# A diffusion backbone layer on one core: the x tiles of the first head group turned to token-major by 32x32 blocks and transfers through DRAM, and its B tile projected last

## The chip, the cores and the metric

The kernel runs on one core of a Trainium2 chip. The core's engines work side by side, each through its own list of instructions: TensorE (matmuls), VectorE, ScalarE and GpSimd; SyncE's queue (SP) issues most transfers between DRAM and the on-chip memory SBUF. Matmuls write to PSUM, from which VectorE or ScalarE take the result. The metric is device microseconds per run; lower is better. An engine that waits for a semaphore holds back everything behind it in its list, and this is as true of the SP queue.

## The reference

One layer works on 512 latent tokens and 256 context tokens of width 1024. Both are normalized, modulated, and multiplied by one wide weight matrix; its columns feed a Mamba-2 mixer (SSD), a windowed attention, and gates. The two branches are merged, and a gated FFN with a convolution follows. What matters here is the SSD's input: columns x (2048, as 4 head groups of 512), B and C (4 groups of 128 states each) go through a convolution of width 3 along the tokens and SiLU.

```python
xbc = jax.nn.silu(dwconv_centred(xbc_raw, conv_w, conv_b))
xs = xbc[..., :D_SSD].reshape(Bsz, L, SSD_GROUPS, SSD_HPG, SSD_HEADDIM)
bm = xbc[..., D_SSD:D_SSD + D_BC].reshape(Bsz, L, SSD_GROUPS, SSD_STATE)
...
states = jnp.einsum('bcsgn,bgrcs,bcsgrp->bcgrpn', bc, decay_to_end, xc)
...
y_diag = jnp.einsum('bgrcls,bcsgrp->bclgrp', scores, xc)
y_off = jnp.einsum('bclgn,bcgrpn,bgrcl->bclgrp', cc, states[:, :-1], jnp.exp(cs))
```

The scan runs in both directions over 4 chunks of 128 latent tokens; it starts from the states that the context's 2 chunks leave. The sums over tokens (`s`) need x and B with tokens on the partitions.

## The kernel before, in words

Every projection is a float32 product made of three matmuls on rounded parts: a weight tile of 128 columns is loaded (`load_raw`, line 177, 512 KB, three buffers `wraw`), ScalarE casts it to the high part `whi` (line 183), VectorE subtracts to get the low part `wlo` (line 184; two buffers of each). `gemm` (lines 237, 238, 240) then multiplies high by high, high by low and low by high for each of 8 slices of the width. Its results have channels on the partitions and tokens along the row: `acc`, 128x512 for latent tokens and 128x256 for context.

For head group g, `proj_steps` makes one step each for B (`b_fn`), C (`c_fn`, latent tokens only) and four x tiles of 128 channels (`x_fn`, called x0 to x3 here). `conv_silu` does the convolution: ScalarE (line 1390), VectorE twice (1391, 1392), ScalarE's tanh (1398), VectorE (1399), all that in one pass for latent and one for context tokens. The result still has channels on the partitions. So each of its 128x128 blocks is turned by TensorE against the identity (`turn`, line 1418) into PSUM, and ScalarE copies the turned tile to `xs` or `xsc` (line 1462), or to `Bk` or `Bkc` for B (line 1439). The turns are not made at once: `TURN` is a list of tiles that wait for one, and `BETWEEN` a list of functions of which `gemm` calls one after every third slice, so that turns and the small matmuls of the scan fall in the middle of the next projection.

`ssd_steps` is the scan of a group. `states` first weighs the context tile `xsc` (line 1491, `xw`), multiplies it by `Bkc` (1520, the state matmuls), copies the state (1522), and then goes back through the latent chunks, where each `advance` (1503 on TensorE, 1505 on GpSimd, 1506 on VectorE) needs a weighed chunk of `xs`. `chunk_in` builds the decay tables E (1593 to 1602) from tables `fb` that are loaded from DRAM, `chunk_out` multiplies E by `xs` (1618). The program goes: projections of group 0; then, per group, its `states`, one gate projection (z15 here for group 0: matmuls, tanh at line 763, VectorE at 765, and a write to DRAM at 766), B of the next group (B1 here), four gate tiles loaded back (1553), a modulation tile m (loaded to `wraw`, used on VectorE at 793 and 795), C of the next group (C1), and the chunks with the x tiles of the next group between them.

In this part the order of the instructions on each engine is set by a scheduler when the program is built, not by the source alone. It is fixed after that. The SP queue's order is set in the same way. Farther on in the program a piece of code (line 1956) turns tiles by VectorE's block transpose and writes them to DRAM block by block (line 1959).

Of the kernel before, what the change touches and what calls it, by code (L numbers as in the profile page):

```python
# [9 lines left out]
F32 = mybir.dt.float32  # L10
# [8 lines left out]
P = 128  # L19
D = 1024  # L20
L = 512
LC = 256
# [22 lines left out]
def tile_hybrid_layer(  # L45
# [31 lines left out]
    nc = tc.nc  # L77
    V, S, G, T = nc.vector, nc.scalar, nc.gpsimd, nc.tensor
# [3 lines left out]
    hpool = ctx.enter_context(tc.tile_pool(name="hpool", bufs=1))  # L82
    tpool = ctx.enter_context(tc.tile_pool(name="tpool", bufs=2))
    dpool = ctx.enter_context(tc.tile_pool(name="dpool", bufs=1, space=DRAM))
# [11 lines left out]
    def bank(name):  # L96
        pool, w = banks_[name]
        return pool.tile([P, 512 * w], F32, tag=name, name=name)
# [8 lines left out]
    def accb():  # L107
        return bank("acc")

    def misb():  # L110
        return bank("mis")
# [3 lines left out]
    def tmp(tag):  # L115
        return tpool.tile([P, 512], F32, tag=tag, name=tag, bufs=TMP[tag])
# [27 lines left out]
    for j, t in enumerate((wdn[0], DSUMS[1], DSUMS[2], DSUMS[5], DSUMS[4], wdn[1], wdn[3])):  # L144
        for u in range(DU):
            n = min(2, DK - 2 * u) * HC
# [82 lines left out]
    BETWEEN = []  # L229

    def gemm(targets, w, nk=KT, m=P, k0=0, first=True, last=True, ks=None):
        hi, lo = w
        for k in range(nk) if ks is None else ks:
            wh, wl = hi[:, k * m : (k + 1) * m], lo[:, k * m : (k + 1) * m]
            a, b = first and k == 0, last and k == nk - 1
            for ps, xh, xl in targets:
                T.matmul(ps, wh, xh[:, k0 + k, :], start=a, stop=False)  # L237
                T.matmul(ps, wh, xl[:, k0 + k, :], start=False, stop=False)  # L238
            for ps, xh, xl in targets:
                T.matmul(ps, wl, xh[:, k0 + k, :], start=False, stop=b)  # L240
            if BETWEEN and k % 3 == 1:
                BETWEEN.pop(0)()
# [24 lines left out]
    dt_d = dpool.tile([64, L + LC], F32, name="dt_d")  # L267
    tt_d = dpool.tile([64, 4], F32, name="tt_d")
    x1_d = dpool.tile([L, D], F32, name="x1_d")
    g2_d = dpool.tile([D], F32, name="g2_d")  # L270

    def col(base, i):
# [152 lines left out]
    with tc.tile_pool(name="spool", bufs=1) as sp:  # L425
# [196 lines left out]
        def put(x, n):  # L622
            r[x] = in_sbuf(B_["s" + x], n, "r_" + x)
# [37 lines left out]
        r = {}  # L661
        cq = tmp("te")[:, :LC]
        for j in range(KT):
# [46 lines left out]
            x = ("hi", "lo") if j >= NU else ("hh", "hl")  # L710
# [31 lines left out]
        for n in range(2):  # L742
            for j in range(KT):
                x = ("hi", "lo") if j >= NU else ("hh", "hl")
# [642 lines left out]
    bp = bpool.enter_context(tc.tile_pool(name="bpool", bufs=1, reuse_waits="tile"))  # L1387

    def conv_half(ps, n, base_w, base_b, i, stride, o):
        S.activation(o[:, :n], ps[:, :n], AF.Identity, scale=hcol(base_w, stride + i), bias=hcol(base_b, i))  # L1390
        V.scalar_tensor_tensor(o[:, 1:n], ps[:, 0 : n - 1], hcol(base_w, i), o[:, 1:n], ALU.mult, ALU.add)  # L1391
        V.scalar_tensor_tensor(o[:, 0 : n - 1], ps[:, 1:n], hcol(base_w, 2 * stride + i), o[:, 0 : n - 1], ALU.mult, ALU.add)

    def conv_silu(ps, n, i, o):
        a = tmp("ta")
        conv_half(ps, n, V_CW, V_CB, i, 24, a)
        t = tmp("tb")
        S.activation(t[:, :n], a[:, :n], AF.Tanh)
        V.scalar_tensor_tensor(o[:, :n], t[:, :n], 1.0, a[:, :n], ALU.add, ALU.mult)

    def flat(a):
        return a.rearrange("p a b -> p (a b)")
# [7 lines left out]
    GR = [{} for _ in range(4)]  # L1410
    TURN = []

    def turn(n=None):

        for t, n_, put in TURN[:n]:
            ps = misb()
            for c in range(n_):
                T.transpose(ps[:, c * P : (c + 1) * P], t[:, c * P : (c + 1) * P], ident)
            put(ps)
        del TURN[:n]  # L1420

    def proj_steps(g):
        d = GR[g]

        def b_fn(w):
            d["xs"] = bp.tile([P, 4, 512], F32, tag="xs", name="xs", bufs=2)
            d["xsc"] = bp.tile([P, 2, 512], F32, tag="xsc", name="xsc", bufs=1)
            d["Bkc"] = bp.tile([P, 2, P], F32, tag="Bkc", name="Bkc", bufs=2)
            d["Bk"] = bp.tile([P, 4, P], F32, tag="Bk", name="Bk", bufs=2)
            d["BT"] = bp.tile([P, L], F32, tag="BT", name="BT", bufs=2)  # L1430
            pl, pc = accb(), accb()
            gemm([LAT(pl)], w)
            turn()
            gemm([CTX(pc)], w)
            conv_silu(pl, L, 16 + g, d["BT"])
            BTc = tmp("tc")
            conv_silu(pc, LC, 16 + g, BTc)
            for t, n, k in ((d["BT"], 4, d["Bk"]), (BTc, 2, d["Bkc"])):
                TURN.append((t, n, lambda ps, n=n, k=k: S.copy(flat(k), ps[:, : n * P])))

        def c_fn(w):
            d["CT"] = bp.tile([P, L], F32, tag="CT", name="CT", bufs=2)
            pl = accb()
            gemm([LAT(pl)], w)
            turn(1)
            conv_silu(pl, L, 20 + g, d["CT"])

        def x_fn(ct, w):
            i = 4 * g + ct
            pl, pc = accb(), accb()  # L1450
            gemm([LAT(pl)], w)
            if not BETWEEN:
                BETWEEN.extend([lambda: None, lambda: turn(1), turn])
            gemm([CTX(pc)], w)
            for pp, n, dst in ((pl, L, d["xs"]), (pc, LC, d["xsc"])):
                xl = tmp("tc")
                conv_silu(pp, n, i, xl)
                TURN.append(
                    (
                        xl,  # L1460
                        n // P,
                        lambda ps, n=n, dst=dst: S.copy(
                            dst[:, :, ct * P : (ct + 1) * P], ps[:, :n].rearrange("p (a b) -> p a b", b=P)
                        ),
                    )
                )

        r = [([("x", 16 + g)], b_fn), ([("x", 20 + g)], c_fn)]
        for ct in range(4):
            r.append(([("x", 4 * g + ct)], lambda w, ct=ct: x_fn(ct, w)))  # L1470
        return r

    SQUARES = []

# [176 lines left out]

    msteps = [m_step(i) for i in range(32)]
    prog = proj_steps(0)
    for g in range(4):
        s = ssd_steps(g)
        f = fill[n2 + g : n2 + 1 + g]
        b = proj_steps(g + 1) if g < 3 else fill[n2 + 4 : n3]
        m = msteps[2 * g : 2 * g + (4 if g == 3 else 2)]

        prog += s[0:1] + f + b[0:1] + s[1:2] + s[10:11] + m[0:1] + b[1:2]  # L1660
        for c in range(4):
            prog += s[2 + 2 * c : 4 + 2 * c] if c < 3 else s[8:9]
            prog += b[2 + c : 3 + c]
            if c == 1:
                prog += b[6:]
            if c == 1 or g == 3:
                prog += m[1 + c : 2 + c] if g == 3 else m[1:2]
        prog += s[9:10]
# [86 lines left out]
    q2 = hpool.tile([P, L], F32, name="q2")  # L1755
# [522 lines left out]
```

## Time and profile before

| | us |
|---|---|
| median of 3 runs (range) | 1220.63 (1220.55 to 1221.63) |
| profiled execution, time | 1221.22 |
| profiled execution, span | 1219.4 |
| TensorE busy | 1211.3 |
| VectorE busy | 924.5 |
| ScalarE busy | 684.4 |
| GpSimd busy | 182.3 |

The sum of busy times is far above the span, since the engines work side by side. A row of the time order has the start, the length, the engine, the source line, the operation and its operands with output first. A row of the groups ends with the total and the mean (in ns), then the idle time before these instructions and what ended it. Lines are those of the kernel before; in the changed kernel the same lines stand one lower from line 270 on, and 28 to 37 lower in and behind the changed functions.

### The profile page before, as it was taken

What the parts mean: (1) busy time and instruction counts of PE and PEld (TensorE: products, weight loads), DVE (VectorE), ACT (ScalarE), POOL (GpSimd) and SP (SyncE); (2) the same over time, 40 slices, a digit from 0 to 9 for tenths busy, and PEclk for the clock granted to TensorE, in tenths of its full rate; (3) what the DMA queues carried; (4) which work ended last, traced back from release to release, by engine and by line L of the source; (5) the groups of instructions that cost most, each with busy time, mean ns of one, the idle gap of its engine ahead of it and who ended that gap; (6) DMA issues with size and microseconds to landing.
All of it is one profiled execution on the core that took longest, in us unless ns stands there. A gap on an engine that the chain in (4) does not pass through costs nothing.

```text
span 1219.4 us, 17443 instructions
## 1 busy us (share of the span) xinstructions
PE 1211.3 (99%) x6320; PEld 995.9 (82%) x6320; DVE 924.5 (76%) x1491; ACT 684.4 (56%) x1271; POOL 182.3 (15%) x183
## 2 busy tenths in 40 slices
PE   9999999999999999999999999999999999999997
PEld 6798888888878877778787778888988888888886
DVE  5857888888564698697896867677687877778778
ACT  5657787788544457476575664223544343436653
POOL 0000121100000043262451632000200000000021
PEclk9999999999999999999999999999999999999999
DMA  9645889844756335357366568777265534336662
GB/s 368 260 138 184 160 242 260 171 149 126 176 160 162 111 117 164 128 125 203 97 159 204 155 209 281 217 248 240 51 162 147 179 115 139 112 122 228 194 182 96
DMA packets 121383, 211.55 MB, mean 173 GB/s; under 512 B 25672, under 2 KB 67728, under 8 KB 121296
## 3 DMA queue, kind: packets, MB, share of 16 engines
q1 hardware_dynamic: 110256, 187.09, 49.4%
q0 software_dynamic: 10752, 23.07, 8.5%
q8 instruction: 50, 0.82, 0.3%
q14 instruction: 37, 0.30, 0.1%
q10 hardware_dynamic: 288, 0.27, 0.1%
HBM read 185.68 MB, written 42.28 MB: 187 GB/s over the span
## 4 chain that ended last, share of the span: by engine, by line
PE 96%; DVE 1%; issue 1%; ACT 1%; DMA 1%; POOL 0%; SPq 0%; POOLq 0%; DVEq 0%; ACTq 0%
PE acc L237 20%; PE acc L240 20%; PE acc L238 20%; PE score L957 3%; PE po L1006 3%; PE pt L993 2%; PE mis L579 2%; PE mis L1610 2%; PE mis L1503 2%; PE mis L1618 1%; PE mis L2137 1%; PE mis L2138 1%; PE mis L2139 1%; PE acc L2137 1%; PE acc L2139 1%; PE acc L2138 1%
## 5 line engine op out<-in xcount | busy, mean ns | idle before, releaser
L183 ACT CAST whi<-wraw 128x1024 fp32r<-128x1024 f32 (+1 forms) x115 | 120.6, 1049 | 158.0 <-PE acc L238 109.5
L184 DVE TENSOR_TENSOR wlo<-wraw,whi 128x1024 fp32r<-128x1024 f32 (+1 forms) x115 | 144.6, 1258 | 68.7 <-ACT whi L183 65.0
L237 PE MATMUL acc<-hlh,whi 128*128 128x512 f32 x472 | 194.2, 411 | 0.0
L238 PE MATMUL acc<-hll,whi 128*128 128x512 f32 x472 | 185.0, 392 | 0.0
L240 PE MATMUL acc<-hlh,wlo 128*128 128x512 f32 x472 | 184.9, 392 | 0.0
L237 PE MATMUL acc<-mh,whi 128*128 128x512 f32 x368 | 143.6, 390 | 0.0
L238 PE MATMUL acc<-ml,whi 128*128 128x512 f32 x368 | 143.2, 389 | 0.0
L240 PE MATMUL acc<-mh,wlo 128*128 128x512 f32 x368 | 143.2, 389 | 0.0
L240 PEld LDWEIGHTS acc<-hlh,wlo 128*128 128x128 f32 x472 | 88.6, 188 | 19.5
L237 PEld LDWEIGHTS acc<-hlh,whi 128*128 128x128 f32 x472 | 88.8, 188 | 17.9 <-issue 3.1
L238 PEld LDWEIGHTS acc<-hll,whi 128*128 128x128 f32 x472 | 88.9, 188 | 17.4 <-issue 2.4
L237 PEld LDWEIGHTS acc<-mh,whi 128*128 128x128 f32 x368 | 69.1, 188 | 14.5
L238 PEld LDWEIGHTS acc<-ml,whi 128*128 128x128 f32 x368 | 69.1, 188 | 14.3
L240 PEld LDWEIGHTS acc<-mh,wlo 128*128 128x128 f32 x368 | 69.1, 188 | 14.2
L1391 DVE SCALAR_TENSOR_TENSOR ta<-acc,half,ta 128x511 f32<-128x511 f32 (+1 forms) x66 | 43.9, 666 | 26.3 <-ACT ta L1390 26.0
L966 DVE CUSTOM_DVE_ANT_0 p<-score,winm,nsink 128x512 f32<-128x512 f32 (+1 forms) x64 | 51.9, 811 | 15.3 <-PE score L957 13.8
L1390 ACT ACTIVATE ta<-acc,half 128x512 f32<-128x512 f32 (+1 forms) x66 | 46.9, 710 | 22.1 <-PE acc L240 20.8
L973 ACT ACTIVATE p<-p,mneg 128x512 f32<-128x512 f32 (+1 forms) x64 | 49.8, 778 | 15.4 <-DVE mneg L966 14.8
L237 PE MATMUL acc<-hch,whi 128*128 128x256 f32 x176 | 54.7, 311 | 0.0
L1505 POOL TENSOR_TENSOR st<-st,eT 128x512 f32<-128x512 f32 x24 | 29.8, 1243 | 165.3 <-ACT st L1522 151.9
L164 POOL DMA_DIRECT2D dsum<-wdn x24 | 25.4, 1144 | 193.0 <-DVE wlo L1090 171.7
L795 DVE SCALAR_TENSOR_TENSOR tm<-wraw,csil,tm 128x512 f32<-128x512 f32 x56 | 44.1, 787 | 13.1 <-DMA wraw<-wm 12.5
(440 smaller groups left out, 2998.2 us busy)
## 6 DMA issues: line engine op xcount, KB each, us to landing
wraw<-wup SPq DMA_DIRECT2D x44, 512.0 KB, 3.7
dsum<-wdn POOLq DMA_DIRECT2D x24, 704.0 KB, 8.5
fb<-cs_d SPq DMA_DIRECT2D x32, 512.0 KB, 6.5
wraw<-wm SPq DMA_DIRECT2D x32, 512.0 KB, 3.9
wraw<-wx SPq DMA_DIRECT2D x24, 512.0 KB, 3.5
wm<-wm SPq DMA_DIRECT2D x16, 512.0 KB, 8.1
wraw<-wz SPq DMA_DIRECT2D x16, 512.0 KB, 3.9
wraw<-wos SPq DMA_DIRECT2D x16, 512.0 KB, 4.8
```

The costliest lines, as they stand in the source:

```text
L183: F["cast"] = S.copy(hi[:, :n], r[:, :n])
L184: return V.tensor_tensor(lo[:, :n], r[:, :n], raw(hi[:, :n]), ALU.subtract)
L237: T.matmul(ps, wh, xh[:, k0 + k, :], start=a, stop=False)
L238: T.matmul(ps, wh, xl[:, k0 + k, :], start=False, stop=False)
L240: T.matmul(ps, wl, xh[:, k0 + k, :], start=False, stop=b)
L795: V.scalar_tensor_tensor(acc, r[:, u * 512 : u * 512 + 512], sc, acc, ALU.mult, ALU.add)
L957: T.matmul(ps[:, o : o + len(z) * P], Q[h][:, b * P : (b + 1) * P], k[:, j, z[0] * P : (z[-1] + 1) * P], start=v == 0 and o % 512 in (0, P ...
L966: V.tensor_tensor_reduce(p[:, :w], d["ps"][i][:, o0 : o0 + w], m, op0=ALU.add, op1=ALU.min, scale=1.0, scalar=nsink[:, h : h + 1], accum_o ...
L973: S.activation(p, p, AF.Exp, bias=d["mneg"][:, i : i + 1], scale=-1.0, accum_out=d["den"][:, i : i + 1])
L1006: T.matmul(d["po"], vst[:, cols[x], j, :], d[y][x], start=x == 0 and y == "pth", stop=x == c - 1 and y == "ptl")
L1390: S.activation(o[:, :n], ps[:, :n], AF.Identity, scale=hcol(base_w, stride + i), bias=hcol(base_b, i))
L1391: V.scalar_tensor_tensor(o[:, 1:n], ps[:, 0 : n - 1], hcol(base_w, i), o[:, 1:n], ALU.mult, ALU.add)
```

## The change

Group 0's x tiles are no longer turned by TensorE. VectorE transposes each convolved tile within blocks of 32x32 (`blocks_out`). Four transfers per tile, one for each 32 channels, write the blocks to a DRAM tensor `xs_d` of tokens by channels. Two loads per tile bring it back as `xs` and `xsc` (`blocks_in`, called in the middle of the next steps for the tiles that are ready). The transfers go out on the SP queue. The steps of group 0 get another order, so that x3 isn't last: x0, C, x1, x2, x3, B in place of B, C, x0 to x3. Groups 1 to 3 stay as they are.

```diff
+    xs_d = [dpool.tile([L + LC, 512], F32, name="xs_d%d" % g) for g in range(4)]
...
+    BY_BLOCKS = (0,)
+
+    def blocks_out(g, ct, n0, n, x):
+
+        t = hpool.tile([P, L], F32, tag="q2" if n == L else "rbc4", name="xb")[:, :n]
+        V.transpose(t, x[:, :n])
+        for a in range(4):
+            c = ct * P + 32 * a
+            o = xs_d[g][n0 : n0 + n, c : c + 32].rearrange("(f i) j -> i f j", i=32)
+            nc.sync.dma_start(o, t[32 * a : 32 * a + 32, :].rearrange("i (f j) -> i f j", j=32))
+
+    def blocks_in(g):
+
+        for ct in READY:
+            c = slice(ct * P, (ct + 1) * P)
+            for x, n0, n in ((GR[g]["xsc"], L, LC), (GR[g]["xs"], 0, L)):
+                nc.sync.dma_start(x[:, :, c], xs_d[g][n0 : n0 + n, c].rearrange("(a p) c -> p a c", p=P))
+        del READY[:]
...
         def b_fn(w):
-            d["xs"] = bp.tile([P, 4, 512], F32, tag="xs", name="xs", bufs=2)
-            d["xsc"] = bp.tile([P, 2, 512], F32, tag="xsc", name="xsc", bufs=1)
+            if not blocks:
+                x_tiles()
...
             gemm([LAT(pl)], w)
             turn()
+            blocks_in(g)
             gemm([CTX(pc)], w)
...
             pl = accb()
+            blocks_in(g)
             gemm([LAT(pl)], w)
             turn(1)
...
         def x_fn(ct, w):
             i = 4 * g + ct
             pl, pc = accb(), accb()
+            if blocks and not ct:
+                x_tiles()
+            blocks_in(g)
             gemm([LAT(pl)], w)
-            if not BETWEEN:
+            if not BETWEEN and not blocks:
                 BETWEEN.extend([lambda: None, lambda: turn(1), turn])
             gemm([CTX(pc)], w)
             for pp, n, dst in ((pl, L, d["xs"]), (pc, LC, d["xsc"])):
                 xl = tmp("tc")
                 conv_silu(pp, n, i, xl)
+                if blocks:
+                    blocks_out(g, ct, 0 if n == L else L, n, xl)
+                    continue
...
+            if blocks:
+                READY.append(ct)
...
-        return r
+        return [r[2], r[1], *r[3:], r[0]] if blocks else r
```

The scheduler's order shifts with it at three places. On the SP queue, this is where the weights of z15 (`wz`) and of B1 (the next `wx`) are asked for before:

```order
L1574 DMA fb_4886<-cs_d_100 128x8x128
L177 DMA wraw_4295<-wx 128x1024
L177 DMA wraw_4377<-wz 128x1024
L177 DMA wraw_4459<-wx 128x1024
L177 DMA wraw_4509<-wm2 128x1024
L1553 DMA zs_4653<-zs_d_97 128x512 x4
L177 DMA wraw_4658<-wx 128x1024
```

And in the changed kernel from x3's last writes on, where `xb_4383` is x3's latent tile and `xb_4397` its context tile, `wraw_4479` holds B1's weights and `wraw_4678` C1's:

```order
L1432 DMA xs_d0_104<-xb_4397 32x8x32 x4
L1439 DMA xs_4028<-xs_d0_104 128x4x128
L177 DMA wraw_4479<-wx 128x1024
L1439 DMA xsc_4029<-xs_d0_104 128x2x128
L767 DMA zs_d_97<-te_4526 128x512
L177 DMA wraw_4529<-wm2 128x1024
L1590 DMA zs_4673<-zs_d_97 128x512 x4
L177 DMA wraw_4678<-wx 128x1024
```

B1's weights now stand behind the block writes of x3 and a load back, and C1's behind z15's gate write, the modulation tile and the gate tiles.

On ScalarE, before, `whi_4461` is B1's high part and `tb_4504` z15's tanh:

```order
L183 CAST whi_4461<-wraw_4459 128x1024
L1462 COPY xsc_4023<-mis_4439 128x2x128
L1390 ACTIVATE ta_4452<-acc_4384,half_90 128x256
L1462 COPY xs_4022<-mis_4472 128x4x128
L1398 ACTIVATE tb_4456<-ta_4452 128x256
L1462 COPY xsc_4023<-mis_4487 128x2x128
L183 CAST whi_4660<-wraw_4658 128x1024
L763 ACTIVATE tb_4504<-acc_4465 128x512
```

In the changed kernel, with `whi_4481` for B1 and `tb_4524` for z15:

```order
L1399 ACTIVATE tb_4476<-ta_4472 128x256
L1467 COPY Bkc_4409<-mis_4507 128x256
L764 ACTIVATE tb_4524<-acc_4485 128x512
L183 CAST whi_4481<-wraw_4479 128x1024
L1559 COPY st_4547<-mis_4544 128x512
```

The cast of B1's weights has moved from well ahead of z15's tanh to right behind it.

On VectorE, the changed kernel between x3 and B1, where `ta_4464` is the convolution of B's latent part, `xb_4397` x3's context tile, `wlo_4482` B1's low part and `tm_4684` the modulation sum:

```order
L1428 STREAM_TRANSPOSE xb_4383<-tc_4375 128x512
L1392 SCALAR_TENSOR_TENSOR ta_4464<-acc_4412,half_90,ta_4464 128x511
L1393 SCALAR_TENSOR_TENSOR ta_4464<-acc_4412,half_90,ta_4464 128x511
L1428 STREAM_TRANSPOSE xb_4397<-tc_4389 128x256
L1400 SCALAR_TENSOR_TENSOR BT_4411<-tb_4468,ta_4464 128x512
...
L766 SCALAR_TENSOR_TENSOR te_4526<-tb_4524,acc_4485 128x512
L1528 TENSOR_TENSOR xw_4520<-xsc_4029,TD_3666 128x512
L184 TENSOR_TENSOR wlo_4482<-wraw_4479,whi_4481 128x1024
L1528 TENSOR_TENSOR xw_4522<-xsc_4029,TD_3666 128x512
L794 TENSOR_SCALAR tm_4684<-wraw_4529,csil_89 128x512
```

Before, the same engine had this there (`wlo_4462` is B1's low part, `wlo_4661` C1's):

```order
L184 TENSOR_TENSOR wlo_4462<-wraw_4459,whi_4461 128x1024
L1391 SCALAR_TENSOR_TENSOR ta_4452<-acc_4384,half_90,ta_4452 128x255
L1392 SCALAR_TENSOR_TENSOR ta_4452<-acc_4384,half_90,ta_4452 128x255
L1399 SCALAR_TENSOR_TENSOR tc_4451<-tb_4456,ta_4452 128x256
L1491 TENSOR_TENSOR xw_4500<-xsc_4023,TD_3662 128x512
L1491 TENSOR_TENSOR xw_4502<-xsc_4023,TD_3662 128x512
L184 TENSOR_TENSOR wlo_4661<-wraw_4658,whi_4660 128x1024
L765 SCALAR_TENSOR_TENSOR te_4506<-tb_4504,acc_4465 128x512
```

x3's context tile is turned behind B's latent convolution, and B1's low part, formerly made ahead of all products on `xsc`, now stands behind the first of them. Beside these places, TensorE's first state matmul for group 0 stands after B1's second matmul and the other one after its fifth (both were after the sixth), C1's low part stands ahead of the first product on `xs`, and two VectorE steps on a later modulation tile, formerly among the first products on `xs`, stand in the first chunk: one ahead of the E products and one between the two.

More of the change, by code (lines that the diff above doesn't have):

```diff
@@ L1420, in turn, with x_tiles, b_fn @@
         del TURN[:n]
+    BY_BLOCKS = (0,)
[12 more added lines that the diff above has]
+        del READY[:]
+    READY = []
     def proj_steps(g):
         d = GR[g]
-        def b_fn(w):
+        blocks = g in BY_BLOCKS
+        def x_tiles():
             d["xs"] = bp.tile([P, 4, 512], F32, tag="xs", name="xs", bufs=2)
             d["xsc"] = bp.tile([P, 2, 512], F32, tag="xsc", name="xsc", bufs=1)
+        def b_fn(w):
+            if not blocks:
+                x_tiles()
             d["Bkc"] = bp.tile([P, 2, P], F32, tag="Bkc", name="Bkc", bufs=2)
```

## The prediction

> **What bounds the kernel now.** I read the page's busy times first, then the chain that ended last, then the stretch that the change touches, engine by engine.
>
> ```profile
> PE 1211.3 (99%) x6320; PEld 995.9 (82%) x6320; DVE 924.5 (76%) x1491; ACT 684.4 (56%) x1271; POOL 182.3 (15%) x183
> PE 96%; DVE 1%; issue 1%; ACT 1%; DMA 1%; POOL 0%; SPq 0%; POOLq 0%; DVEq 0%; ACTq 0%
> 365.85:421.92 56.07, 56.07 (x320) 48.97 (x318) 30.49 (x44) 27.53 (x52) 0.00 (x0) 1.00 0.50 144
> ```
>
> The first two lines are the busy times and the shares of the chain. TensorE is the bound, and the chain runs through it for 96% of the span. The third is the busy time of each engine in one stretch: its length, then PE, PEld, DVE, ACT and POOL, the granted clock, the DMA share and GB/s. The stretch reaches from the first matmul of the B tile of group 0 to the first of the B tile of group 1 (B1 below). TensorE is busy through all of it at full clock. So a TensorE instruction removed there saves its time, and a TensorE wait added there costs its time; work on VectorE (30.49 of 56.07 us) or ScalarE costs only what it makes TensorE wait.
>
> **What TensorE loses.** The change takes 24 of the 30 turns of 128x128 in this stretch (four channel tiles, four latent and two context blocks each); B's own six stay. Their price comes from the lengths of tiles without turns in the order of time on TensorE:
>
> ```profile
> 365.85 0.39 PE L237 MATMUL acc<-hlh,whi 128*128 128x512 f32 x1
> 371.32 0.28 PE L237 MATMUL acc<-hch,whi 128*128 128x256 f32 x1
> 374.19 0.40 PE L237 MATMUL acc<-hlh,whi 128*128 128x512 f32 x1
> 379.66 0.60 PE L1418 MATMUL mis<-ident,BT 128*128 128x128 f32 x4
> 421.92 0.39 PE L237 MATMUL acc<-hlh,whi 128*128 128x512 f32 x1
> ```
>
> B or x (latent and context part) takes 374.19 - 365.85 = 8.34 us, a latent part alone 379.66 - 374.19 = 5.47 us. The stretch holds five of the first (B, x0 to x3) and two of the second (C and z15): 41.70 + 10.94 = 52.64 us. The remaining 56.07 - 52.64 = 3.43 us are the 30 turns, 0.114 us each, so 24 are 2.74 us. That is the most that can be gained, 0.22%. Without any wait B1 would start at 421.92 - 2.74 = 419.18; call this moment T. The four and four copies out of PSUM (L1462) leave ScalarE, which has 28 us of slack there: nothing.
>
> **What the new road costs.** The kernel has the same road elsewhere already: line 1956 turns a tile in 32x32 blocks on VectorE and line 1959 writes it in four transfers of 64 KB. Its rows are the turn, the issue on the SP queue (min/median/max ns), the time from issue to landing, and the landing of other transfers:
>
> ```profile
> L1956 DVE STREAM_TRANSPOSE te<-x 128x512 f32<-128x512 f32 x8 | 5.6, 704 | 0.0
> L1959 SPq DMA_DIRECT2D x_d<-te x32: 303/480/1637, 865.9 to 940.9; - x32
> DMA to landing us min/median/max: 1.7/3.7/4.8
> wraw<-wx SPq DMA_DIRECT2D x24, 512.0 KB, 3.5
> wraw<-wm SPq DMA_DIRECT2D x32, 512.0 KB, 3.9
> zs<-zs_d SPq DMA_DIRECT2D x16, 256.0 KB, 4.5
> zs_d<-te SPq DMA_DIRECT2D x16, 256.0 KB, 2.6
> khi<-khi SPq DMA_DIRECT2D x6, 192.0 KB, 3.0
> ```
>
> VectorE gains four turns of 0.70 us and four of half the width (0.35 to 0.45, an estimate from the same row), 4.4 us in a stretch where it idles 25 us: hidden by that idle time. The SP queue gains 32 writes and 8 loads back, 40 x 0.48 = 19 us of issue, and each load back stops the queue until its block writes have landed. What is queued behind them are weight loads. Those for B and z15 are issued late but find room: before, the queue asked for B1's weights 24 us ahead of their cast, as the next rows show. The end of x3 has no such room.
>
> ```profile
> 391.10 0.33 SPq L177 DMA_DIRECT2D wraw<-wx  x1
> 415.55 1.04 ACT L183 CAST whi<-wraw 128x1024 fp32r<-128x1024 f32 x1
> 422.85 0.59 ACT L763 ACTIVATE tb<-acc 128x512 f32<-128x512 f32 x1
> 371.52 0.78 ACT L1390 ACTIVATE ta<-acc,half 128x512 f32<-128x512 f32 x1
> 373.12 0.75 DVE L1392 SCALAR_TENSOR_TENSOR ta<-acc,half,ta 128x511 f32<-128x511 f32 x1
> ```
>
> *B1's weights.* Before, they were cast (L183) 6 us before use. Now the cast stands behind z15's gate activation (L763) on ScalarE, and that waits for z15's last matmul. ScalarE starts 0.20 us after TensorE's last matmul of a tile (371.32 to 371.52), so B1's first matmul cannot start before T + 0.20 + 0.59 + 1.04 = T + 1.83 us. The order of the instructions forces this wait; it takes two thirds of the gain.
>
> *The context tile xsc.* Now VectorE's split of B1's weights (wlo) stands behind the first product on xsc (L1491). So follow xsc. The context block turn of x3 stands behind both convolution steps of B's latent part. That part ends a context part (374.19 - 371.32 = 2.87), z15 (5.47) and six turns (0.69) before T: T - 9.03. Convolution ends 373.12 + 0.75 - 371.32 = 2.55 later, the turn 0.4 after it: T - 6.1. The fourth write is issued three times 0.48 and 0.1 later, T - 4.5. It lands by the rows of x_d 1.7, 3.7 or 4.8 us later. Then the load back is issued, 128 KB, by the nearest rows 3.0 (khi) to 4.5 us (zs), 3.5 in the middle. So xsc is there at T + 0.2, T + 2.7 or T + 4.8.
>
> ```profile
> L1491 DVE TENSOR_TENSOR xw<-xsc,TD 128x512 f32<-128x512 f32 x16 | 10.6, 690 | 4.4 <-ACT xsc L1462 3.8 <-PE mis L1520 0.3
> L184 DVE TENSOR_TENSOR wlo<-wraw,whi 128x1024 fp32r<-128x1024 f32 x112 | 141.5, 1263 | 65.8 <-ACT whi L183 62.2 <-PE mis L1503 2.2 <-PE mis L1618 0.7
> 422.14 0.39 PE L238 MATMUL acc<-hll,whi 128*128 128x512 f32 x1
> 423.28 1.88 PE L1520 MATMUL mis<-xw,Bkc 128*128 128x512 f32 x4
> 424.59 0.79 PE L237 MATMUL acc<-hlh,whi 128*128 128x512 f32 x1
> 425.23 0.40 PE L238 MATMUL acc<-hll,whi 128*128 128x512 f32 x1
> 430.87 1.02 PE L1503 MATMUL mis<-xw,Bk 128*128 128x512 f32 x2
> ```
>
> Middle: 2.7 + 0.69 (product) + 1.23 (the split here; its mean is 1.26) = T + 4.6. The first matmul that needs wlo is B1's third, now with one state matmul ahead of it: 0.46 for two matmuls, (424.59 - 423.28) / 2 = 0.65 for the state, 0.41 for the matmul after an f32 one (425.23 - 424.59 = 0.64 in place of 422.14 - 421.92 = 0.22): T + 1.5 if nothing waited. Wait 3.1 us, which takes in the 1.83 above. The ends: T + 0.2 leaves the 1.83 alone; T + 4.8 makes it 5.2. I take the middle, since 3.7 is the median over 32 writes of the same form. The two state matmuls are now apart, so that one more matmul pays the step after f32: +0.41.
>
> *C1's weights* come next on the SP queue, behind z15's gate write, a modulation tile (m) and four gate tiles:
>
> ```profile
> 399.92 0.33 SPq L177 DMA_DIRECT2D wraw<-wm  x1
> 400.30 1.84 SPq L1553 DMA_DIRECT2D zs<-zs_d  x4
> 404.76 13.45 SPq L177 DMA_DIRECT2D wraw<-wx  x3
> 403.46 0.49 DVE L793 TENSOR_SCALAR tm<-wraw,csil 128x512 f32<-128x512 f32 x1 [1.69 <-DMA wraw<-wm]
> ```
>
> The gate's VectorE step ends at about T + 1.6; then 0.4 for each issue, and C1's load is issued at T + 4.3 (m and zs took 400.30 + 1.84 - 399.92 = 2.2 us). It comes after 1.5 MB and lands 3.5 us later by its own row, or up to 5.5 (an estimate: the 4.5 of zs, behind which it is queued, and 1 us more), T + 7.8 to T + 9.8. Cast, split and the product of the third chunk follow on ScalarE and VectorE: + 1.05 + 1.26 + 0.69 = T + 10.8 to T + 12.8. That product feeds the first advance of the state (L1503), due without waits at T + 430.87 - 421.92 + 0.41 = T + 9.36. Wait 1.4 to 3.4 us; it doesn't add to the 3.1, since it is counted from T too: the later of the two decides. The m tile lands about T + 6, and its two VectorE steps (0.49 and 0.75) end before the third state matmul is due with the wait of 3.1: nothing.
>
> *VectorE in the first chunk.* Two steps on the next m tile (L795) fell before into a wait of VectorE for data (second row). Now they stand ahead of and between the products on E (L1602), with no idle time to take them:
>
> ```profile
> 436.44:446.38 9.94, 9.94 (x55) 7.03 (x54) 9.77 (x17) 7.85 (x17) 3.49 (x4) 1.00 0.36 107
> 428.35 0.75 DVE L795 SCALAR_TENSOR_TENSOR tm<-wraw,csil,tm 128x512 f32<-128x512 f32 x1 [2.35 <-DMA wraw<-wm]
> 442.49 1.50 DVE L1602 TENSOR_TENSOR E<-E,mis 128x512 f32<-128x512 f32 x2
> 444.25 1.09 PE L1618 MATMUL mis<-E,xs 128*64 128x128 f32 x16
> ```
>
> VectorE is busy 9.77 of 9.94 us there (first row). They push the second E by 2 x 0.75 = 1.5 us. Before, it was ready at 443.99 and first used half way through the 16 matmuls, at 444.8: 0.8 us of room. TensorE itself is later by the sum so far and VectorE by a little less, so 0 to 0.9 us are lost; I take 0.5.
>
> **The sum**, against the profiled execution (span 1219.4, time 1221.22, 0.6 above the median 1220.63 of the runs): -2.74 + 3.1 + 0.41 + 0.5 = +1.3 us. On the median that is 1221.9 us. From the ends: -2.74 + 1.83 + 0.41 = -0.5, or 1220.1; -2.74 + 5.2 + 0.41 + 0.9 = +3.8, or 1224.4. A measurement of this kernel can tell about 0.2%, 2.4 us, from no change.
>
> **Rivals.** *All hidden:* weights and xsc are in time, the 2.74 us stay, 1217.9. For it speaks that the DMA engines have room; against it the cast behind the gate, which costs 1.83 whatever lands when. Chance 4%.
>
> *Slower, by landing times:* the place is the last block write of x3 and the load back. If together they take over 8.4 us (7.2 in the forecast), xsc comes after T + 3.9, and the wait exceeds 4.3, which is what turns the sum above +2.4. At the rows' maximum it gives 1224.4. For it: 4.8 was reached in x_d, and the load back is queued right behind B1's 512 KB. Against it: the engines are otherwise little used there.
>
> ```profile
> 407.00:415.00 8.00, 8.00 (x49) 7.09 (x48) 4.66 (x7) 3.25 (x6) 0.00 (x0) 1.00 0.31 102
> ```
>
> The DMA share before is 0.31 in this stretch. Chance 36%.
>
> *Strided writes one after another:* if the four writes of a tile do not overlap, the last lands 3 x 4.8 = 14 us later and the sum is 14 us worse than its middle, 1236. Against it, writes of x_d were issued 0.48 apart and none took over 4.8. Chance 2%. [...]
>
> **How the numbers follow.** The forecast, with xsc between T and T + 3.9 and so a change of -0.5 to +2.4 us, has the remaining 58%; its time is 1221.9. Faster by over 0.2% is the first rival alone, 0.04. Slower by over 0.2% is the second and third, 0.38. The rest, 0.58, lies within. The range goes from 1219.9, just below the forecast's lower end, to 1224.9, above the second rival's end; outside lie the first and third rival and a tail of the second.
>
> **What would show it.** In the changed profile: L1418's successor with 24 fewer turns by B1's start; ScalarE's gate and then the cast right before B1; TensorE idle 2 to 4 us at B1's first three matmuls, with VectorE's wlo or xw named; xw waiting for the DMA into xsc; a second wait, if any, at the first advance, put down to C1's wraw; block writes landing in 2 to 5 us. It is wrong if B1 waits under 1.8 us, if xsc lands after T + 5, if weights of B or z15 come late too, or if the time is lost or gained outside 365 to 450 us.

## The result, and the profile after

The changed kernel takes 1226.05 us (median of 6 runs, 1224.3 to 1227.1), the kernel before beside it 1220.68 us. The ratio is 1.0041, with a 95% interval of 1.0028 to 1.0054: slower by 0.41%, 1.15 us above the upper end of my range. The profiled execution took 1225.21 us (span 1223.4), 3.99 us more than the profiled one of before.

The first two lines are the busy times and the shares of the chain, from the page of the changed kernel. The third is the same stretch as in the prediction: from the first matmul of group 0's first projection (B before, x0 now) to the first of B1.

```profile
PE 1210.0 (99%) x6296; PEld 993.3 (81%) x6296; DVE 925.4 (76%) x1499; ACT 679.5 (56%) x1263; POOL 183.7 (15%) x183
PE 93%; ACT 2%; DVE 2%; DMA 1%; issue 1%; POOL 0%; SPq 0%; POOLq 0%; DVEq 0%; ACTq 0%
366.12:421.26 55.14, 53.52 (x295) 46.30 (x293) 31.13 (x49) 24.75 (x44) 0.00 (x0) 1.00 0.59 146
```

TensorE has 24 instructions less and 1.3 us less to do, yet its share of the chain fell from 96 to 93%, and VectorE's and ScalarE's rose from 1 to 2% each. The stretch is only 0.93 us shorter than before (55.14 for 56.07) though 2.74 us of turns are gone: it now ends with a wait of 1.62 us, 1.78 when counted from T (below). The waits of TensorE from 360 to 480 us (engine and line that waits, what for, total, times, longest); before, there was none in these 120 us:

```profile
PE mis L1540 <- DVE xw L1528: 2.1, 1, 2.1
PE acc L237 <- ACT whi L183: 1.6, 1, 1.6
PE mis L1557 <- DVE xw L1528: 1.4, 1, 1.4
```

Line 1540 is the advance of the state, 1557 the state matmuls, 1528 the products on xsc and xs. How they come about is read from four engines, in the order of time. First the SP queue, where 1432 is a block write, 1439 a load back, 767 z15's gate write and 1590 the gate tiles:

```profile
409.95 5.14 SPq L1432 DMA_DIRECT2D xs_d<-xb  x7
415.26 0.38 SPq L1439 DMA_DIRECT2D xs<-xs_d  x1
415.68 0.50 SPq L177 DMA_DIRECT2D wraw<-wx  x1
416.34 0.36 SPq L1439 DMA_DIRECT2D xsc<-xs_d  x1
421.02 0.33 SPq L767 DMA_DIRECT2D zs_d<-te  x1
421.40 0.43 SPq L177 DMA_DIRECT2D wraw<-wm  x1
421.87 2.07 SPq L1590 DMA_DIRECT2D zs<-zs_d  x4
424.05 3.98 SPq L177 DMA_DIRECT2D wraw<-wx  x3
```

B1's weights are asked for at 415.68, 24.6 us later than before (391.10); C1's are the first of the three at 424.05, 19.3 us later than before (404.76). Then ScalarE and VectorE:

```profile
419.68 0.60 ACT L764 ACTIVATE tb<-acc 128x512 f32<-128x512 f32 x1 [1.72 <-PE acc L240]
420.17 1.04 ACT L183 CAST whi<-wraw 128x1024 fp32r<-128x1024 f32 x1
430.63 1.05 ACT L183 CAST whi<-wraw 128x1024 fp32r<-128x1024 f32 x1 [5.16 <-DMA wraw<-wx]
420.31 0.69 DVE L766 SCALAR_TENSOR_TENSOR te<-tb,acc 128x512 f32<-128x512 f32 x1 [3.66 <-ACT tb L764]
420.92 0.68 DVE L1528 TENSOR_TENSOR xw<-xsc,TD 128x512 f32<-128x512 f32 x1
425.95 0.94 DVE L794 TENSOR_SCALAR tm<-wraw,csil 128x512 f32<-128x512 f32 x1 [2.61 <-DMA wraw<-wm]
427.59 1.29 DVE L1528 TENSOR_TENSOR xw<-xsc,TD 128x512 f32<-128x512 f32 x2
431.71 1.22 DVE L184 TENSOR_TENSOR wlo<-wraw,whi 128x1024 fp32r<-128x1024 f32 x1 [2.83 <-ACT whi L183]
432.85 2.15 DVE L1528 TENSOR_TENSOR xw<-xs,TD 128x512 f32<-128x512 f32 x2
```

And TensorE, only its rows with a wait:

```profile
421.26 0.50 PE L237 MATMUL acc<-hlh,whi 128*128 128x512 f32 x1 [1.62 <-ACT whi L183]
428.33 1.98 PE L1557 MATMUL mis<-xw,Bkc 128*128 128x512 f32 x4 [1.42 <-DVE xw L1528]
434.45 1.13 PE L1540 MATMUL mis<-xw,Bk 128*128 128x512 f32 x2 [2.07 <-DVE xw L1528]
```

ScalarE's gate starts at 419.68, so T (the prediction's moment when z15 ends) is 0.20 before it, 419.48. Three things follow. B1's cast stands right behind the gate, and B1 starts at T + 1.78. The first product on xsc starts at 420.92 right behind the gate's VectorE step, with no wait named: the tile from DRAM was there by T + 1.4. But the modulation tile is there only at 425.95, and two products on xsc are queued behind its two steps; and C1's weights are there at 430.63, 6.6 us after their issue, and the first products on xs are queued behind C1's split.

The chain that ended last shows which of these decided. Behind z15's gate it leaves the compute engines (start, length, what):

```profile
421.02 0.33 SPq L767
...
424.05 6.56 DMA wraw<-wx
430.63 1.06 ACT whi L183
...
432.85 1.55 DVE xw L1528
434.45 1.13 PE mis L1540 x2
```

It runs from the gate's write through the issues of the modulation tile and of the gate tiles (between the first two rows) to C1's load, C1's cast and split, and the first product on xs. Neither x3's way through DRAM nor the waits before it on TensorE are in it. Before, C1's load (404.76) stood ahead of the gate's write (424.83) on the SP queue; now it stands behind it.

The first advance stands at 434.45, before it stood at 430.87: + 3.58 us. That is - 2.74 (turns) + 0.27 (the stretch began later) + 1.62 + 1.42 + 2.07 (waits), and 0.94 that is left for the additional steps after f32 matmuls and after waits (each wait is counted from the end of the last matmul's row, not from the moment when the next could have begun). It stays: the E products come 3.69 us later (447.94 for 444.25), the end 4.0.

### The profile page after: what moved, and what is told of

It is laid out like the page before. It is cut to its first block, busy times and chain, and to the rows that moved or that the text cites. A ratio compares the mean times of both kernels' runs of the same rounds, so it can differ in the third digit from the quotient of the medians.

```text
span 1223.4 us, 17455 instructions
## 1 busy us (share of the span) xinstructions
PE 1210.0 (99%) x6296; PEld 993.3 (81%) x6296; DVE 925.4 (76%) x1499; ACT 679.5 (56%) x1263; POOL 183.7 (15%) x183
## 4 chain that ended last, share of the span: by engine, by line
PE 93%; ACT 2%; DVE 2%; DMA 1%; issue 1%; POOL 0%; SPq 0%; POOLq 0%; DVEq 0%; ACTq 0%
PE acc L237 19%; PE acc L240 19%; PE acc L238 19%; PE score L958 3%; PE po L1007 3%; PE mis L580 2%; PE pt L994 2%; PE mis L1647 2%; PE mis L1540 2%; PE mis L1655 1%; PE mis L2174 1%; PE mis L2175 1%; PE mis L2176 1%; PE acc L2174 1%; PE acc L2176 1%; PE acc L2175 1%
## 5 line engine op out<-in xcount | busy, mean ns | idle before, releaser
L238 PEld LDWEIGHTS acc<-ml,whi 128*128 128x128 f32 x368 | 69.1, 188 | 14.2
L1391 ACT ACTIVATE ta<-acc,half 128x512 f32<-128x512 f32 (+1 forms) x66 | 46.7, 708 | 24.6 <-PE acc L240 23.3
L1002 DVE TENSOR_TENSOR ptl<-pt,pth 128x512 fp32r<-128x512 f32 x72 | 47.5, 685 | 9.1 <-ACT pth L998 7.9
```

What stands on the lines that cost most here:

```text
L1002: V.tensor_tensor(d["ptl"][x], d["pt"][x], raw(d["pth"][x]), ALU.subtract)
```

## The experiments

Two theories stood against each other at first. The *queue theory*: what costs the time is that the weight loads (and the modulation tile) are now issued late, since the SP queue has them behind transfers that wait. The *trip theory*: TensorE waits for x3's own way through DRAM. A third, the *order theory*, put it down to the new order of the projections. The kernel before had medians of 1221.1, 1220.91 and 1221.4 us in the three batches (runs e1 to e4, e5 to e8, e9 and e10).

| run | edit | median us (range) | ratio to before, 95% |
|---|---|---|---|
| changed kernel | | 1226.05 (1224.3 to 1227.1) | 1.0041 (1.0028 to 1.0054) |
| e1 | gate tiles behind C1's weights | 1224.8 (1224.01 to 1227.55) | 1.0035 (1.0022 to 1.0047) |
| e2 | x3 turned by TensorE | 1219.65 (1219.15 to 1221.38) | 0.9989 (0.998 to 0.9998) |
| e3 | transfers issued by GpSimd | 1220.88 (1220.33 to 1222.28) | 1.0 (0.9991 to 1.0009) |
| e4 | order of steps alone | 1220.97 (1220.72 to 1221.4) | 0.9999 (0.999 to 1.0007) |
| e5 | late weight loads alone | 1222.63 (1222.16 to 1223.62) | 1.0013 (1.0004 to 1.0022) |
| e6 | C between x3 and B | 1233.84 (1233.11 to 1234.9) | 1.0106 (1.0092 to 1.012) |
| e7 | no turning at all | 1218.17 (1217.91 to 1218.99) | 0.9978 (0.9969 to 0.9987) |
| e8 | the changed kernel again | 1225.5 (1224.47 to 1227.84) | 1.0041 (1.0027 to 1.0055) |
| e9 | B1's and C1's weights by GpSimd | 1222.9 (1222.18 to 1223.34) | 1.0012 (1.0004 to 1.0021) |
| e10 | gate tiles loaded twice | 1228.43 (1227.35 to 1230.18) | 1.0058 (1.0044 to 1.0072) |

**Is it the order of steps, or the price of a turn?** e4 is the kernel before, with the steps of group 0 in the new order and all turns left on TensorE. e7 is the changed kernel without the block turns and writes; it leaves work out and serves as a yardstick only.

```diff
-        return r
+        return [r[2], r[1], *r[3:], r[0]] if g == 0 else r
```

> The kernel before with only the order of group 0's steps changed (x0, C, x1, x2, x3, B), every turn on TensorE. Queue and trip theory: no cost in the order itself, within 1 us of before, 1219.7 to 1221.7. Order theory: 1223 or more.

```diff
-                    blocks_out(g, ct, 0 if n == L else L, n, xl)
...
-                nc.sync.dma_start(x[:, :, c], xs_d[g][n0 : n0 + n, c].rearrange("(a p) c -> p a c", p=P))
+                nc.sync.dma_start(x[:, :, c], x1_else[ct][:, : n].rearrange("p (a c) -> p a c", c=P))
```

> Leaves out the turning of group 0's x tiles altogether: no block turns, no writes of blocks; the eight loads into the token-major tiles stay, but read an input, so nothing waits for anything written. The ceiling of the change: 24 turns less at 0.114 us are 2.74 us, 1218.0 to 1218.6 us by either theory. If it is above 1220, the price of a turn on TensorE, or the new order's own cost, was read wrongly.

e4 is 1220.97, the time of before, with no wait that before hasn't: the order alone costs nothing. e7 is 1218.17, 2.74 us below the 1220.91 beside it, where the prediction had 24 x 0.114 = 2.74. That it fits to the hundredth is luck: the interval of the ratio allows 1.6 to 3.8 us. So the gain was sized rightly as far as this can tell, and the changed kernel loses 7.9 us against e7 (1226.05 - 1218.17) by what the blocks' way brings with it.

**Queue or trip?** e3 issues the same block writes and loads back from GpSimd's list, so that the SP queue has its old order. In e9 they stay on SP, and only the loads of B1's and C1's weights go to GpSimd.

```diff
-            nc.sync.dma_start(o, t[32 * a : 32 * a + 32, :].rearrange("i (f j) -> i f j", j=32))
+            nc.gpsimd.dma_start(o, t[32 * a : 32 * a + 32, :].rearrange("i (f j) -> i f j", j=32))
...
-                nc.sync.dma_start(x[:, :, c], xs_d[g][n0 : n0 + n, c].rearrange("(a p) c -> p a c", p=P))
+                nc.gpsimd.dma_start(x[:, :, c], xs_d[g][n0 : n0 + n, c].rearrange("(a p) c -> p a c", p=P))
```

> The same transfers, writes and loads back, issued by GpSimd instead of the SP queue; the SP queue then has the order of the kernel before. Queue theory: B1, modulation tile and C1 are in time; what stays is at most the wait for xsc itself, so 1218 to 1220. Trip theory: xsc still makes its way and GpSimd issues slower, 1224 to 1228. Order theory: about 1225.

```diff
-        dma = nc.sync.dma_start(r[:, :n], a)
+        q = nc.gpsimd if key in (("x", 17), ("x", 21)) else nc.sync
+        dma = q.dma_start(r[:, :n], a)
```

> The changed kernel, its block writes and loads back all on the SP queue as before; only the two weight loads of B1 and C1 are issued by GpSimd, whose list is empty there, so that they no longer stand behind anything. Queue theory: B1's weights arrive early, the waits at B1's first matmul (1.6 us) and for C1's chain at the first advance (2.1 to 3.1 us) go, and 1218.5 to 1221.5 us result, the upper end if the modulation tile, which stays on SP behind z15's gate, still holds VectorE. Trip theory (x3's way through DRAM is what TensorE waits for): the trip is unchanged, so 1224 us or more.

e3 came out at 1220.88, 5.2 us below the changed kernel and 0.9 above the upper end that the queue theory gave; the trip theory is out by over 3 us. On GpSimd's list the trip is in fact slower. Line 1432's rows (issue, then landing, each min/median/max) of the changed kernel, and then of e3:

```profile
L1432 SPq DMA_DIRECT2D xs_d<-xb x32: 302/458/2360, 376.6 to 414.6; - x32
DMA to landing us min/median/max: 1.5/1.7/6.2
```

```profile
L1432 POOL DMA_DIRECT2D xs_d<-xb x32: 585/618/694, 376.3 to 414.9; - x32
DMA to landing us min/median/max: 1.9/4.1/6.4
```

A block write takes 4.1 us to land instead of 1.7, and yet 5.2 us are won: the length of the trip isn't what costs them. In e3, C1's load goes out at 404.96, ahead of the gate's write at 421.74, as before. Beside the queue's order, e3 changes the orders on ScalarE and VectorE too, since the scheduler puts B1's cast and split ahead of z15's gate again; e3 alone doesn't tell the two apart.

The trip isn't free. e3's remaining waits in that stretch are 0.9 us at the state matmuls and 0.3 at the first advance, both for products on xsc or xs. Its span is 1.5 us longer than e7's (1218.7 for 1217.2), and its median 2.7. So of the 7.9 us that the changed kernel loses against e7, e3 wins back 5.2; what makes up the other 2.7 is shown for 1.2 only.

e9 missed both expectations: 1222.9, 1.4 above the queue theory's upper end and 1.1 below the trip theory's bound. The two waits that it was to remove are gone (0.2 us are left at an advance). But the scheduler put xsc's load back behind z15's gate write and the modulation tile, and the products on xsc behind B1's convolution. The SP queue of e9 (768 is the gate write, 1440 the load back), and its waits of TensorE:

```profile
420.51 0.34 SPq L768 DMA_DIRECT2D zs_d<-te  x1
420.90 0.43 SPq L178 DMA_DIRECT2D wraw<-wm  x1
421.53 0.37 SPq L1440 DMA_DIRECT2D xsc<-xs_d  x1
```

```profile
PE mis L1656 <- ACT tb L1400: 1.1, 2, 0.6
...
PE mis L1656 <- DVE E L1640: 0.6, 1, 0.6
```

VectorE then has no idle time from 430 to 436, and the E products (1656) of this and of the next chunks come late. xsc's loads land 3.5 to 4.0 us after their issue in e9, so xsc was there by 425.5; the first product on it began at 427.26, behind the convolution's steps on VectorE. So e9 moved more than two weight loads, and it is no clean test of either theory.

**Do late weight loads alone cost time?** e5 has no blocks: it is e4 with one more rule, that B1's weights may not be asked for before B's SiLU.

```diff
...
+        if key == ("x", 17):
+            tc.add_manual_dep(dma.ins, F["bt", 0].ins.name, BEHIND, reason="late weights")
...
```

> No blocks at all: the kernel before in the order x0, C, x1, x2, x3, B, all turns on TensorE, and one thing more: B1's weight load may not be issued before B's latent SiLU result exists, so that it, the modulation tile, the gate tiles and C1's weights are asked for as late as in the changed kernel. Queue theory (late weight loads alone cost TensorE time): C1's load is issued a few us behind z15's gate write as in the changed kernel, TensorE waits 1 to 3 us at the first advance and for the modulation tile's sake at the third state matmul, 1222 to 1224 us, with no gain from turns. Trip theory (the wait is for x3's way through DRAM): nothing travels, so 1220.5 to 1221.7, as the kernel before.

1222.63, 1.66 us above e4, whose order of steps it shares: within the queue theory's range, and the trip theory (nothing travels) is out. Its mechanism was not quite what I wrote. The waits that the profile names are small (0.4 us for B1's wlo, 0.2 at the E products), not 1 to 3 us at the first advance; C1's load is issued at 419.25 there, before the gate's write (424.11) and not behind it, and lands 6.9 us later. So e5 delays the loads by less than the change does, and shows that late loads cost time, not that they cost all of it. The E products are 0.86 us later than in e4 (445.81 for 444.95 at the advance behind them), and where the other half of the 1.5 us in the spans (1220.6 for 1219.1) goes isn't shown by the waits.

**More time for the trip.** e6 lets x3 travel during a whole projection more.

```diff
-        return [r[2], r[1], *r[3:], r[0]] if blocks else r
+        return [*r[2:], r[1], r[0]] if blocks else r
```

> The changed kernel with the steps of group 0 in the order x0, x1, x2, x3, C, B, so that one more projection lies between x3 and the use of its tiles. Trip theory: x3 is back long before B1, the waits go, 1218.5 to 1219.5 us. Queue theory: what matters is what the SP queue asks for when; here B's own weights now stand behind x3's block writes, so TensorE waits at B instead, by some 3 to 8 us, and 1222 to 1230 us result though x3 has more time.

It is the slowest of all, 1233.84. The one large wait is at group 0's own B. The wait, and the SP queue ahead of it:

```profile
PE acc L237 <- ACT whi L183: 12.1, 1, 12.1
```

```profile
407.52 0.38 SPq L1439 DMA_DIRECT2D xsc<-xs_d  x1
407.94 3.61 SPq L1432 DMA_DIRECT2D xs_d<-xb  x7
411.66 0.39 SPq L177 DMA_DIRECT2D wraw<-wx  x1
```

TensorE had nothing to do from 404.81 on. The queue issued x3's writes, the last at 411.5, since these had to wait for x3's convolution and block turns; B's weights were next, at 411.66. One order of transfers that suits x3 starves TensorE, and the trip theory's 1218.5 to 1219.5 is 14 us off. The direction was the queue theory's; its wait of 3 to 8 us and its 1230 us at most were too little.

**One load out of the way.** e1 puts the four gate tiles behind C1's weights, and e10 doubles them ahead of it.

```diff
-        prog += s[0:1] + f + b[0:1] + s[1:2] + s[10:11] + m[0:1] + b[1:2]
+        prog += s[0:1] + f + b[0:1] + s[1:2] + (s[10:11] if g else []) + m[0:1] + b[1:2] + ([] if g else s[10:11])
```

> Only the place of the four gate tiles' loads of group 0 changes: they are asked for behind C1's step, so C1's weights (and the next x tile's) go out right behind the modulation tile. Queue theory (B1's, the modulation tile's and C1's loads are late on the SP queue, and TensorE waits for their casts): C1's weights land about 3 us earlier, the 2.1 us wait at the first advance shrinks to under 0.5, the waits at B1's start (1.6) and at the third state matmul (1.4) stay; about 1224, 2 us under the changed kernel. Trip theory (the last context tile's way through DRAM sets the end of the waits): no change, 1226. Order theory (B last, and the blocks' load on VectorE): no change, 1226.

```diff
-            for ct in range(4):
+            for k in range(4 if g else 8):
+                ct = k % 4
...
-                if ct == 0:
+                if k == 0:
```

> The changed kernel with group 0's four gate tiles loaded twice over, so that C1's weights stand behind 1 MB and four issues more. Queue theory: C1's weights land 2 to 3.5 us later and the wait at the first advance grows by as much, to 4 to 6.6 us, nothing else changing: 1227.5 to 1229.5 us. If a wait of over 4 us also lowers TensorE's granted clock, as the 12.1 us wait of the run with C behind x3 did, some 2.5 us come on top: 1229.5 to 1232 us and a mean clock of 0.997 or less. If C1's landing doesn't matter: 1224.3 to 1227.8 us.

In e1, C1's weights are issued at 421.38 and land 4.9 us later instead of 6.6, and the wait at the first advance is gone. But its median, 1224.8, lies above the 1224 that I gave it. The wait came back one step earlier, since C1's split now stands ahead of the last product on xsc:

```profile
427.41 1.23 DVE L184 TENSOR_TENSOR wlo<-wraw,whi 128x1024 fp32r<-128x1024 f32 x1 [0.78 <-ACT whi L183]
428.55 1.54 DVE L1528 TENSOR_TENSOR xw<-xsc,TD 128x512 f32<-128x512 f32 x1
```

```profile
430.15 1.12 PE L1557 MATMUL mis<-xw,Bkc 128*128 128x512 f32 x2 [2.35 <-DVE xw L1528]
```

The first row is C1's split; it waits for C1's cast, and the product that TensorE needs waits behind it. The first advance stands at 433.19, T + 14.2 (T is 418.99 there), against T + 15.0: 2.07 us of wait removed bring 0.8.

In e10, 1228.43, C1's load is issued 5.6 us later than in the changed kernel and its wait becomes 4.17 us, at the third advance, since the scheduler now has two products on xs ahead of C1's split. The median lies in the range that I gave without a lowered clock (1227.5 to 1229.5), but four of the five executions have a mean clock of 0.995 to 0.997, which I had put with the higher range: the two ranges didn't separate the cases. The profiled execution, 1230.18 us, shows the lowered clock, to which the last section comes back.

**The changed kernel again.**

> The changed kernel once more, unaltered, for a second profile. Both theories: 1224.3 to 1227.1 us, as before. If the landing times of transfers set its waits, the waits at B1, at the third state matmul and at the first advance differ between the two profiles by some tenths to 2 us, and the span with them; if a fixed order sets them, they are equal to 0.2 us.

```profile
PE mis L1540 <- DVE xw L1528: 3.1, 1, 3.1
PE acc L237 <- ACT whi L183: 1.6, 1, 1.6
PE mis L1557 <- DVE xw L1528: 1.1, 1, 1.1
```

1225.5 us. The wait for B1's cast is the same to 0.1 us, since a fixed order sets it. The other two differ by 0.3 and 1.0 us: they hang on when a transfer lands (the modulation tile took 4.0 us instead of 4.6, C1's weights 7.2 instead of 6.6).

**A better version.** e2 takes three x tiles by blocks and leaves x3, the one with no time, to TensorE.

```diff
...
+            blocks = order and ct < 3
...
```

> x0 to x2 by blocks, x3 turned by TensorE again (six turns back), B still last. Queue theory: nothing on the queue waits for x3, B1's and C1's weights are asked for some 10 us earlier, the three waits go; 18 turns saved are 2.05 us, so 1218.6 to 1219.2. Trip theory: the same 1218.6 to 1219.2, since the last trip is gone as well. Order theory: three quarters of VectorE's load and the whole new order stay, so over 1223.

1219.65, 0.45 us above the upper end that the queue and the trip theory gave, ratio 0.9989 (0.998 to 0.9998): the only complete kernel here that beats the one before, by 0.11%, just clear of no change. It can't tell the two theories apart, since x3's trip is gone too. There is no wait of TensorE from 360 to 480 us, and the first advance stands at 428.88, 1.99 us earlier than before (18 turns are 2.05). B1's weights are issued at 405.29, the modulation and gate tiles behind them and C1's weights at 409.00, all ahead of z15's gate write (421.47).

## Why the prediction was wrong

The sign was right, and so was the mechanism in outline (turns gained, weight loads late, waits at B1 and at the first advance). The size was not: +5.4 us on the median for +1.3. The step that failed is C1's chain: the sum held its wait to 1.4 to 3.4 us and let the wait for xsc, 3.1 us, decide; in the trace it delayed the first advance by 5.6 us, and the wait for xsc didn't exist.

- *The turns, 2.74 us.* Right: e7 gained 2.74.
- *B1's weights, T + 1.83.* Right: B1 starts at T + 1.78. This is the one wait that the order of instructions forces, and the surest term.
- *The context tile, wait 3.1 from xsc at T + 2.7.* Wrong. The product on xsc started at 420.92 without a wait, so xsc was there by T + 1.4, near my early end. I took 3.7 us for the landing of the last write from x_d's rows of 64 KB; the last write here has 32 KB, and the median over all of xs_d is 1.7. The loads into xsc then landed in 2.3 to 3.7 us. So the wait of 1.83 alone stood there, and the forecast's middle rested on a term that did not exist.
- *The modulation tile, nothing.* Wrong, and for the same reason. It lands at T + 6.5, where I had T + 6; but it was hidden only by the wait of 3.1 that didn't come. TensorE waited 1.42 us for it, which C1's chain then took in.
- *C1's chain, T + 10.8 to T + 12.8.* This is the term that failed. Issue at T + 4.6 (T + 4.3 predicted) was nearly right. The landing took 6.6 us, 7.2 in e8, where my bounds were 3.5 and 5.5. The product behind the split took 1.55 us, not 0.69. The first advance came at T + 15.0, 5.6 us after it was due without waits; I had 1.4 to 3.4. Against my upper end, T + 12.8, these 2.2 us are 0.3 from the issue, 1.1 from the landing and 0.9 from the product, each rounded. The product's price could have been read before, where the second product on xs has it:

```profile
430.28 1.55 DVE L1491 TENSOR_TENSOR xw<-xs,TD 128x512 f32<-128x512 f32 x1
```

  The DMA share shows why 5.5 was no upper bound. The columns are as in the prediction's stretches, DMA share and GB/s last:

```profile
421.50:423.50 2.00, 2.00 (x7) 1.05 (x7) 1.84 (x3) 0.00 (x0) 0.00 (x0) 1.00 0.80 227
423.50:425.50 2.00, 2.00 (x9) 1.30 (x8) 0.00 (x0) 0.59 (x1) 0.00 (x0) 1.00 0.95 316
425.50:427.50 2.00, 1.41 (x7) 0.82 (x5) 1.52 (x2) 0.00 (x0) 1.06 (x1) 1.00 0.98 355
427.50:429.50 2.00, 1.17 (x3) 0.67 (x4) 1.38 (x3) 0.00 (x0) 0.00 (x0) 1.00 1.03 412
```

  From 421.4 on the queue asks for the modulation tile, four gate tiles, C1 and two more weights in 6.6 us, 3 MB. I had read the share of 0.31 from 407 to 415 of the kernel before, and took a transfer's own row plus 1 us; but the change puts together what stood apart before. e1, with 1 MB less ahead, has 4.9 us.
- *"The later of the two decides."* That form was right: the waits at B1 and for the modulation tile don't add to C1's chain, since the chain that ended last passes them by (ScalarE waited 5.16 us for C1's transfer, VectorE then 2.83 for its cast). I had the wrong one as the decider: of the signs that I named, the product waiting for xsc didn't show, and the second wait, put down to C1's load, did.
- *The additional step after f32, 0.41, and E, 0.5.* The step and its kind measured 0.94. E cost 0.1 us (3.69 for 3.58).
- *The rival "slower, by landing times"* (36%) gave 1224.4, the nearest of the times, but by xsc, which was in time. Its place was wrong, and its price was that of another transfer. *Strided writes one after another:* didn't happen; the writes landed in 1.7 us at the median. *All hidden:* no; e7 shows what that would be.

The profiled executions account for 4.0 us. The medians differ by 5.4. What is between them is not read from a profile of the changed kernel itself; the last section has what points to it.

## What to carry to other kernels

The SP queue handed its waits on to what stood behind (in e6, where B's weights stood behind x3's block writes, TensorE waited 12.1 us): before work is moved to transfers, list what is queued behind the first transfer that must wait, and cost that, not the trip. The loads that a wait held back were then issued together, so the landing time of one alone was no bound for them (C1's took 6.6 us, where the median of its row was 3.5); take it from a stretch with the same bytes queued. And move only those tiles whose way ends well before their use: with three of the four tiles the kernel won 1.45 us against the one before it, with all four it lost 5.4.

## What the runs showed of the hardware

*In e10 a wait of 4.17 us cost about 3 us more, by estimate.* TensorE's last matmul ended at 435.73 and the next began at 439.90. The granted clock is the figure ahead of the last two:

```profile
438.00:438.50 0.50, 0.00 (x0) 0.00 (x0) 0.50 (x2) 0.00 (x0) 0.00 (x0) 1.00 0.14 57
438.50:439.00 0.50, 0.00 (x0) 0.00 (x0) 0.50 (x2) 0.00 (x0) 0.00 (x0) 0.82 0.00 0
...
445.00:445.50 0.50, 0.50 (x3) 0.40 (x2) 0.50 (x1) 0.50 (x3) 0.50 (x1) 0.50 0.00 0
445.50:446.00 0.50, 0.50 (x4) 0.42 (x3) 0.50 (x2) 0.50 (x3) 0.50 (x1) 0.85 0.00 0
```

It fell from 1.00 to 0.50 at 438.82 (by slices of 0.1 us), 3.1 us after the last matmul, and came back at 445.65, 5.75 us after the first. In e6 it fell at 409.11, 4.3 us after the last matmul, and came back at 422.76, 5.84 us after the first. At half clock for 5.75 us some 2.9 us are lost, by estimate. The waits of 2.07 and 3.06 us in the changed kernel's two profiles left it at 1.00.

Fall and return lie 6.83 us apart in e10 and 13.65 in e6. Why the clock fell 1.2 us sooner behind the last matmul in e10 than in e6, no run shows.

The lowered clock points to what the profiles of the changed kernel don't show. Of e1's five executions the three at 1224.01 to 1224.8 us have a mean clock of 0.999, the two at 1226.77 and 1227.55 have 0.996. Of the eleven of the changed kernel, the five up to 1225.5 have 0.998 to 0.999, the six from 1225.97 on 0.997 to 0.998. A wait that varies around 3 us (2.07 and 3.06 in the two profiles), and lowers the clock in some executions as the 4.17 us did in e10, would do that, and would lift the median over the profiled execution. That it did so in those executions is argued, not shown: none of them was profiled with its clock low.

*VectorE beside GpSimd.* Three VectorE products of two SBUF tiles that began while GpSimd's product of the state ran took 1.54 to 1.55 us instead of 0.69 and ended 0.54 to 0.55 us after GpSimd's: in the changed kernel at 432.85 and in e1 at 428.55, with GpSimd's running from 432.24 to 433.85 and from 427.94 to 429.54, and in the kernel before at 430.28, with GpSimd's from 429.66 to 431.29. Products that began first kept 0.68 (436.29 and 438.53 in the changed kernel, GpSimd's from 436.45 and 438.69), and so did a convolution step that reads `acc` from PSUM its 0.74 (436.89).

*The block writes* into `xs_d`, of 32 or 64 KB with 32 numbers together, landed in 1.7 us at the median from the SP queue, and in 4.1 when GpSimd issued them (e3).
